# Order changes in a one-core decoder layer: which half of a modulation piece is multiplied first, and where splits, key sums and gate loads stand

## The chip, the cores and the metric

The kernel runs on one core of a Trainium2 chip. The metric is the device time of one launch in microseconds (us), the median of several runs. The core has a matrix engine (TensorE, PE in the profile, with its weight loads on a row PEld), three elementwise engines (VectorE or DVE, ScalarE or ACT, GpSimd or POOL), and a sequencer that mainly issues transfers (SyncE, SP). Each engine works through its own list of instructions in order; they meet through semaphores. Transfers (DMAs) are issued by SP, ACT and POOL.

## The reference

One layer of a decoder for 512 prompt tokens and 8 sample tokens, which share all weights (D = 1024, 16 heads of 64, feed-forward width 2816):

```
sh1, sc1, g1, sh2, sc2, g2 = split(silu(c) @ ada_w + ada_b, 6)
h = rms_norm(x, norm1_g) * (1 + sc1) + sh1
xr, gr, q, k, v, fl, ga, gb = split(h @ w_in)
xc = causal_dwconv(xr);  hr = rg_lru(xc)           # gates: 16 blocks of 64 x 64
ya = (hr * gelu(gr)) @ w_proj_a
yb = attend(q, k, v, log_sigmoid(fl + b_f)) @ w_proj_b
x = x + g1 * ((sigmoid(ga) * ya + sigmoid(gb) * yb) @ w_o)
h2 = rms_norm(x, norm2_g) * (1 + sc2) + sh2
x = x + g2 * ((silu(gu) * up) @ w_ffn_out)         # gu, up = split(h2 @ w_ffn_in)
y = rms_norm(x, normf_g)
```

The prompt attends causally to itself. Each sample token attends to 1024 past rows in pages of 128 rows (`cache_k`, `cache_v`, found through a page table), with a decay from the stored forget values.

## The kernel before

All activations are kept transposed, features on the 128 partitions and the 520 tokens (512 + 8) along the free axis, in two halves of 260. A product of 128 output features is 8 steps over the features of the input, each with three matmuls: weights and activations are both split into a rounded part and the rest (`whi`, `wlo`; `hh`, `hl`), and hi·hi + lo·hi + hi·lo is summed. A weight chunk arrives as `wraw` (L210); for each 128 columns of it, a *unit*, ACT rounds it to `whi` (L246) and DVE subtracts to get `wlo` (L248). `split_upto(n)` (it starts with `while state["split"] <= n`) does this ahead of the product; units 0 and 1 are the weights of q's last two tiles, units 2 and 3 those of the first two tiles of `xr`. `held(m)` puts the subtraction of unit m behind an instruction named in `after[m]`.

The program is written as Python that emits instructions, and a scheduler lays them out per engine by its own estimate of times; `tc.issue_after(i)` tells it to place what follows behind instruction i. That layout is fixed at build time.

Four places matter here.

**q's tiles** (the loop with `q_done`). Tiles 0 to 5 were half computed earlier (`qpart`); their second half goes into a bank `q{i}_{j}`, and DVE adds it to `qp` (L921). `q_done` then copies the 8 sample columns on POOL (L876), writes the tile to DRAM (`qd`, L878) and transposes the sample columns on PE (L879, bank `qt`). After the fourth tile ACT scales the bank (L885) and writes it out as `qtd` (L188). POOL reads it back for one sample, spread over all partitions, as `qb` (L714). In the same loop `forget_logits` (`pfl`), `past_turn` (`lft`), `decay` and `past_conv` (the small `lzc` and `cvp` operations on DVE) are issued.

**Key pages.** POOL issues loads of key pages (`pg`, L696). `key_sum` multiplies a page by `qb` (L740, L744) and sums over each head (L741, L745) on DVE, two DVE instructions of 128x1024 each.

**Gates.** `gate_load(i)` loads the block weights of one tile (`gw`, L903); ACT and DVE split them (L908, L909).

**adaLN pieces.** The modulation for the second half of the layer is `silu(c) @ ada_w`, in 16 pieces (`ada_piece`, L370): two groups `ada1`, `ada2` of 8 input steps. A piece has two loads of 512 KB (`ada_load`, L358, tile `araw`, from a pool of 7 buffers), and each load feeds two matmul calls with 32 output partitions; the four calls of a piece write to four different column groups of the array (`tile_position=(0, 32 * g)`). Each call is two MATMUL records in the trace. The calls are placed among the products `pb` and `wo`; `ada_copy` and `ada_end` turn the sums into `mod`.

Every DMA from SP or ACT raises one of eight semaphores (DMAHW0 to DMAHW7, taken in turn), and waits until the DMA that had the same one before has landed. POOL's DMAs use DMASW0 to DMASW7 in the same way.

Of the kernel before, what the change touches and what calls it, by code (L numbers as in the profile page):

```python
# [12 lines left out]
ALU = mybir.AluOpType  # L13
# [11 lines left out]
KT = 8  # L25
# [3 lines left out]
HALF = NT // 2  # L29
# [36 lines left out]
def kernel(ctx, tc, xT, par, gates, b_f, cst, cse, own, cache_k, cache_v, cache_lf, pt,  # L66
# [3 lines left out]
    pe, act, dve, pool, sp = nc.tensor, nc.scalar, nc.vector, nc.gpsimd, nc.sync  # L70
# [9 lines left out]
    def slot(name, cols=NT, dt=F32, parts=128):  # L80
        return heap.tile([parts, cols], dt, name=name, tag="slot")
# [77 lines left out]
    for jt in range(FF // 128):  # L159
        c = len(chunks)  # L160
# [4 lines left out]
        for name in BLOCKS:  # L165
            units.append((c, name, 4))
            if name in JOIN[jt]:
                g, i = JOIN[jt][name]
# [12 lines left out]
    state = {"n": 0, "dma": 0, "split": 0, "load": 22, "lead": 11, "due": 0, "age": 1}  # L181
# [35 lines left out]
    after = {}  # L217
# [132 lines left out]
    ada_raw = {}  # L350
# [10 lines left out]
    def ada_piece(which, kq):  # L361
        if kq == 0:
            ada_acc[which] = bank(f"ada{which}")
        acc = ada_acc[which]
        if (which, kq) not in ada_raw:
            ada_load(which, kq)
        for g2, raw in enumerate(ada_raw.pop((which, kq))):
            for gg in range(2):
                g = 2 * g2 + gg
                pe.matmul(acc[32 * g:32 * g + 32, :], lhsT=silc[:, kq], rhs=raw[:, gg],  # L370
                          start=kq == 0, stop=kq == KT - 1, tile_position=(0, 32 * g))
# [174 lines left out]
    for f in range(KT):  # L546
        t = slot("sq1")
# [14 lines left out]
    for f in range(KT):  # L562
        t = slot("xn")
# [163 lines left out]
    def key_sums():  # L727
        for p in pend:
            p[0] += 1
        while pend and pend[0][0] >= (state["age"] if state["n"] < 43 else 1000):  # L730
            key_sum()

    def key_sum():
        _, s, j, pg, q, half = pend.pop(0)
        r = s // 2
        c = 256 * (r % 2) + 32 * j + H * (s % 2)
        with tc.issue_after(state["last"].ins):
            if half is not None:
                b, c = 8 * (r % 2) + j, H * (s % 2) + 8 * half
                dve.tensor_tensor(pg, pg, q.unsqueeze(1).to_broadcast([128, 2, 512]), ALU.mult)  # L740
                dve.tensor_reduce(S[r // 2].rearrange("p (b c) -> p b c", c=32)[:, b:b + 2, c:c + 8],  # L741
                                  pg.rearrange("p j (h d) -> p j h d", d=DH), AX.X, ALU.add)
            else:
                dve.tensor_tensor(pg, pg, q, ALU.mult)  # L744
                last = dve.tensor_reduce(S[r // 2][:, c:c + H], pg.rearrange("p (h d) -> p h d", d=DH), AX.X, ALU.add)  # L745
        summed[r] += 1
        if summed[r] == 2 * NPAGE:
            chains.append([9, past_softmax(r)])
        return None if half is not None else last

    def key_pages(n):
        for _ in range(n):
            if keys_todo:
                key_page(*keys_todo.pop(0))
# [119 lines left out]

    def q_done(i, t):
        c = pool.tensor_copy(q8[:, NS * i:NS * i + NS], t[:, NP:])  # L876
        state.setdefault("q8", c)
        sp.dma_start(qd[i], t)  # L878
        pe.transpose(qtp[i // 4][:, 128 * (i % 4):128 * (i % 4) + 128], t[:, NP:], ident)  # L879
        if i % 4 == 3:  # L880
            q_samples(i // 4)
# [17 lines left out]
    gate_raw = {}  # L899

    def gate_load(i):
        gate_raw[i] = slot("gw", 256)
        sp.dma_start(gate_raw[i], gates[i])  # L903

    def gate_split(i):
        gr = gate_raw.pop(i)
# [5 lines left out]
    for i in range(KT):  # L912
        if i % 4 == 0:
            qtp.append(bank(f"qt{i}", NS))
        if i < 6:
            t = qpart[i]
            for j, (t0, t1) in enumerate(HALVES):
                b = bank(f"q{i}_{j}")
                for k in range(4):
                    q_matmuls(1, i, j, k, b)  # L920
                dve.tensor_tensor(t[:, t0:t1], b[:, :HALF], t[:, t0:t1], ALU.add)  # L921
        else:
            t = slot("q")
            product(f"q{i}", h, to(t, act.copy))
        if ready:
            q_done(*ready.pop())
        ready.append((i, t))
        if i == 2:
            flw = forget_weights()
        if i == 3:  # L930
            split_upto(0)
            for n in range(KT):
                gate_load(n)
        if i in (5, 6):
            for n in (2 * i - 10, 2 * i - 9):
                gate_split(n)
        if i == 4:
            with tc.issue_after(state["q8"].ins):
                past_load()
            split_upto(1)  # L940
            load_chunks(1)
            loads[pool] += [state["hr"]] * 4
            key_pages(2)
            with tc.issue_after(state["last"].ins), tc.issue_after(state["act"].ins):
                decay()
                past_conv()
            close = forget_logits(flw)
        if i == 5:
            past_turn(0)
            past_turn(1)  # L950
            key_pages(2)
        if i == 6:
            close()
            load_chunks(2)
        if i == 3:
            q_done(*ready.pop())
    q_last = ready.pop()
# [816 lines left out]
```

## Time and profile before

| what | value |
|---|---|
| runs | 1035.36, 1036.88, 1037.04 us; median 1036.88 |
| the profiled execution's own time | 1032.73 us |
| its span, first to last instruction | 1031.1 us |
| mean granted TensorE clock | 0.995 |
| busy: PE, DVE, ACT, POOL | 1003.5, 794.0, 548.5, 325.1 us |

Rows of the timeline read: start in us from the span's start, duration in us, engine, line, operation, output<-inputs, count, and in brackets the engine's idle time before it with what ended it. Matmuls are pipelined: each record lasts 0.28 us, but in a full stream they start 0.12 us apart, so that the cost of a disturbance is read from the starts. "SPq" and the like are DMA issues. The waits view says who waited for whom: us in total, times, longest. The chain of waits follows the last instruction of a window back through what released each step.

### The profile page before, as it was taken

The page shows a single profiled execution, that of the slowest core. Times are in us where ns is not written, and L with a number is a line of the kernel's source. Part 1 is how long each engine was busy: PE and PEld are TensorE (multiplying, and loading weights), DVE is VectorE, ACT ScalarE, POOL GpSimd, SP SyncE. Part 2 cuts the span into 40 slices and gives each one's busy share as a digit, 9 for nine tenths or more (in the row PEclk, how much of TensorE's full clock was granted, in tenths as well). Part 3 has the DMA queues.
Part 4 walks back from the last instruction along what each step waited for, and adds up shares of the span by engine and source line. Part 5 has one row for each costly group of instructions (what it writes and reads, how often), then busy time and mean ns, then how long its engine had stood idle before and what let it go on. Part 6 is the DMA issues. An engine that isn't in the chain of part 4 may idle for free.

```text
span 1031.1 us, 21277 instructions
## 1 busy us (share of the span) xinstructions
PE 1003.5 (97%) x8012; PEld 923.6 (90%) x8012; DVE 794.0 (77%) x1423; ACT 548.5 (53%) x1128; POOL 325.1 (32%) x416
## 2 busy tenths in 40 slices
PE   5998999999999999999999999999999999999996
PEld 2788999999998988888888877999999999999996
DVE  5548999998999888887655443868878888878865
ACT  4524575847671477777783222555444444445453
POOL 0335211111144146554400000483432433424212
PEclk9999999999999999999999999999999999999998
DMA  9796867778889999987867894324243342333122
GB/s 327 240 318 208 245 228 180 245 247 269 280 260 334 326 320 292 312 271 237 266 199 280 318 341 140 84 63 118 68 124 94 91 123 65 100 103 103 62 63 84
DMA packets 164377, 206.97 MB, mean 201 GB/s; under 512 B 9890, under 2 KB 125106, under 8 KB 164210
## 3 DMA queue, kind: packets, MB, share of 16 engines
q1 hardware_dynamic: 147554, 152.52, 47.6%
q0 software_dynamic: 13040, 46.67, 13.8%
q10 hardware_dynamic: 3680, 6.42, 1.7%
q8 instruction: 63, 1.03, 0.4%
q14 instruction: 40, 0.33, 0.1%
HBM read 192.49 MB, written 13.09 MB: 199 GB/s over the span
## 4 chain that ended last, share of the span: by engine, by line
PE 89%; DMA 4%; DVE 3%; ACT 1%; issue 1%; POOL 1%; SPq 0%; DVEq 0%; POOLq 0%; ACTq 0%
PE fo L305 12%; PE wo L305 5%; PE k L305 5%; PE gb L305 5%; PE gr L305 5%; PE pb L305 5%; PE ga L305 5%; PE v L305 4%; PE xr L305 4%; PE pv L833 3%; PE pa L305 3%; PE ada L370 2%; PE po L1288 2%; PE qp L538 2%; PE ptt L1254 2%; PE fi L305 1%
## 5 line engine op out<-in xcount | busy, mean ns | idle before, releaser
L246 ACT CAST whi<-wraw 128x1024 fp32r<-128x1024 f32 (+1 forms) x79 | 82.0, 1038 | 113.6 <-PE pb L305 34.5
L248 DVE TENSOR_TENSOR wlo<-wraw,whi 128x1024 fp32r<-128x1024 f32 (+1 forms) x79 | 99.6, 1261 | 24.1 <-ACT whi L246 21.8
L270 ACT CAST wb<-ws 128x512 fp32r<-128x512 f32 x72 | 44.8, 622 | 93.5 <-PE fo L305 64.4
L305 PE MATMUL fo<-ach,wb 128*128 128x260 f32 x512 | 93.3, 282 | 0.0
L696 POOL DMA_DIRECT2D pg<-in_cache_k_dram x74 | 39.8, 537 | 151.3 <-DVE S L745 62.5
L271 DVE TENSOR_TENSOR wb<-wraw,wb 128x512 fp32r<-128x512 f32 x86 | 76.6, 891 | 5.7 <-ACT wb L270 4.5
L305 PEld LDWEIGHTS fo<-ach,wb 128*128 128x128 f32 x512 | 79.0, 188 | 0.0
L261 POOL TENSOR_TENSOR ws<-wraw 128x512 f32<-128x512 f32 x18 | 23.9, 1330 | 157.8 <-DMA wraw<-in_w_fi_dram 81.2
L270 ACT CAST wb<-wraw 128x512 fp32r<-128x512 f32 x86 | 53.5, 622 | 36.3 <-ACT cp L1663 6.3
L305 PE MATMUL fo<-acl,wb 128*128 128x260 f32 x256 | 72.3, 282 | 0.0
L271 DVE TENSOR_TENSOR wb<-ws,wb 128x512 fp32r<-128x512 f32 x72 | 59.6, 828 | 14.8 <-ACT wb L270 13.0
L744 DVE TENSOR_TENSOR pg<-pg,qb 128x1024 f32<-128x1024 f32 x48 | 58.0, 1223 | 2.3 <-DMA pg<-in_cache_k_dram 2.2
L745 DVE TENSOR_REDUCE S<-pg 128x16 f32<-128x1024 f32 x48 | 57.3, 1207 | 0.2
L1245 POOL TENSOR_SCALAR p<-p,mu 128x128 f32<-128x128 f32 (+3 forms) x28 | 38.7, 1393 | 51.7 <-DVE mu L1241 45.6
L305 PEld LDWEIGHTS fo<-acl,wb 128*128 128x128 f32 x256 | 48.1, 188 | 0.0
L1239 ACT ACTIVATE p<-p,mu 128x128 f32<-128x128 f32 (+3 forms) x64 | 35.4, 554 | 17.8 <-DVE mu L1238 17.5
L305 PE MATMUL xr<-hh,wlo 128*128 128x260 f32 x128 | 37.1, 290 | 2.1 <-DVE wlo L248 2.1
L305 PE MATMUL v<-hh,whi 128*128 128x260 f32 x128 | 37.3, 291 | 0.8 <-ACT row L813 0.5
L305 PE MATMUL pb<-oh,whi 128*128 128x260 f32 x128 | 37.2, 291 | 0.3 <-ACT oh L1346 0.3
L305 PE MATMUL xr<-hh,whi 128*128 128x260 f32 x128 | 37.4, 292 | 0.0
L305 PE MATMUL k<-hh,whi 128*128 128x260 f32 x128 | 37.3, 291 | 0.0
L305 PE MATMUL gb<-hh,whi 128*128 128x260 f32 x128 | 37.0, 289 | 0.0
(1101 smaller groups left out, 3969.5 us busy)
## 6 DMA issues: line engine op xcount, KB each, us to landing
araw<-in_ada_w_dram SPq DMA_DIRECT2D x48, 512.0 KB, 7.9
wraw<-in_w_fi_dram SPq DMA_DIRECT2D x44, 512.0 KB, 4.2
pg<-in_cache_k_dram POOLq DMA_DIRECT2D x42, 512.0 KB, 6.0
pg<-in_cache_v_dram SPq DMA_DIRECT2D x42, 512.0 KB, 5.4
wraw<-in_w_in_dram SPq DMA_DIRECT2D x34, 512.0 KB, 7.2
wraw<-in_w_in_dram SPq DMA_DIRECT2D x11, 1024.0 KB, 8.8
pg<-in_cache_v_dram POOLq DMA_DIRECT2D x22, 512.0 KB, 6.2
pg<-in_cache_k_dram POOLq DMA_DIRECT2D x32, 256.0 KB, 5.3
```

The costliest lines, as they stand in the source:

```text
L246: state["act"] = act.copy(hi[:, :k1 - k0], src)
L248: state["last"] = dve.tensor_tensor(lo[:, :k1 - k0], src, hi[:, :k1 - k0].bitcast(F32), ALU.subtract)
L261: pool.tensor_tensor(s1, a21, a22, ALU.add)
L270: state["act"] = act.copy(t[:, :4], src)
L271: state["last"] = dve.tensor_tensor(t[:, 4:], src, t[:, :4].bitcast(F32), ALU.subtract)
L305: state["mm"] = pe.matmul(out[:, :t1 - t0], lhsT=wt[k], rhs=at, start=k == 0 and m == 0, stop=k == nk - 1 and m == 2)
L696: done.append(eng.dma_start(pg, cache[bass.ds(r, 1), :, c0:c1].rearrange("a p c -> (a p) c")))
L744: dve.tensor_tensor(pg, pg, q, ALU.mult)
L745: last = dve.tensor_reduce(S[r // 2][:, c:c + H], pg.rearrange("p (h d) -> p h d", d=DH), AX.X, ALU.add)
L833: pe.matmul(pv[0][32 * gq:32 * gq + 32, :], lhsT=pw[r][:, c:c + 32], rhs=pgs[gq // 2][:, 512 * hf:512 * hf + 512], start=j == 0, stop=j == ...
L1239: act.activation(p[:, :n + 128], p[:, :n + 128], AF.Exp, bias=mu[:, 0:1], scale=-1.0, accum_out=mu[:, 1:2])
L1245: (pool.tensor_scalar(p, p, mu[:, 2:3], None, ALU.mult) if a and i + 1 < KT else act.activation(p, p, AF.Copy, scale=mu[:, 2:3]))
```

## The change

Five edits, all of them in the order of things; no operation is added or taken away but that eight gate loads become four.

1. A piece of adaLN multiplies its second load first (`for g2 in (1, 0)`), then its first; before, it took them in the order of loading.
2. The DVE subtractions of units 0 and 1 (q's last two tiles) are put behind the second of the two sums of q's third tile.
3. Key sums are put behind the latest of the sums of q's tiles 0 to 5 (`state["qadd"]`).
4. `past_load` waits as before for the first tile's copy on POOL; four loads of key pages that come after the sixth tile are put behind the copy of the fourth tile.
5. Gates are loaded two at a time, one load of 256 KB each: the first after q's fourth tile, the second after the sixth, the last two after the seventh. Before, all eight loads were issued after the fourth.

```
@@ ada_piece
-        for g2, raw in enumerate(ada_raw.pop((which, kq))):
+        raws_ = ada_raw.pop((which, kq))
+        for g2 in (1, 0):
+            raw = raws_[g2]
             for gg in range(2):
@@ key_sums
-            key_sum()
+            with tc.issue_after(state["qadd"].ins):
+                key_sum()
@@ q_done
-        state.setdefault("q8", c)
+        if i in (0, 3):
+            state["q8"] = c
@@ gate_load
-        gate_raw[i] = slot("gw", 256)
-        sp.dma_start(gate_raw[i], gates[i])
+        t = slot("gw", 512).rearrange("p (g c) -> p g c", g=2)
+        sp.dma_start(t, gates[i:i + 2].rearrange("g p c -> p g c"))
+        gate_raw[i], gate_raw[i + 1] = t[:, 0], t[:, 1]
@@ the loop over q's tiles
-                dve.tensor_tensor(t[:, t0:t1], b[:, :HALF], t[:, t0:t1], ALU.add)
+                state["qadd"] = dve.tensor_tensor(t[:, t0:t1], b[:, :HALF], t[:, t0:t1], ALU.add)
+                if i == 2:
+                    after[0] = after[1] = state["qadd"]
...
+        if i == 1:
+            first_q8 = state["q8"]
...
         if i == 3:
             split_upto(0)
-            for n in range(KT):
-                gate_load(n)
+            gate_load(0)
+        if i == 5:
+            gate_load(2)
...
-            with tc.issue_after(state["q8"].ins):
+            with tc.issue_after(first_q8.ins):
                 past_load()
...
             key_pages(2)
+            loads[pool] += [state["q8"]] * 4
         if i == 6:
             close()
             load_chunks(2)
+            gate_load(4)
+            gate_load(6)
```

What the edits and the scheduler make of it, engine by engine (lines of the changed kernel are 2 to 13 higher):

PE's list is the same up to the product `wo`. There, inside the stream of the `wo` tiles, six of the sixteen adaLN pieces (the last six) stood as two separate pairs of calls; the other ten stood together already. Before, for the first of the six (`araw_9037` and `araw_9039` are its two loads; `x2` in a row stands for two calls):

```order
L305 MATMUL wo1_0_9055<-mixh_8516,whi_8917 128x260
L305 MATMUL wo1_0_9055<-mixh_8516,wlo_8918 128x260
L370 MATMUL ada2_8978<-araw_9037,silc_99 32x512 x2
L305 MATMUL wo1_0_9055<-mixl_8517,whi_8917 128x260
L305 MATMUL wo1_0_9055<-mixh_8591,whi_8917 128x260
L305 MATMUL wo1_0_9055<-mixh_8591,wlo_8918 128x260
L305 MATMUL wo1_0_9055<-mixl_8592,whi_8917 128x260
L305 MATMUL wo1_0_9055<-mixh_8664,whi_8917 128x260
L305 MATMUL wo1_0_9055<-mixh_8664,wlo_8918 128x260
L370 MATMUL ada2_8978<-araw_9039,silc_99 32x512 x2
L305 MATMUL wo1_0_9055<-mixl_8665,whi_8917 128x260
```

And now (`araw_9029` and `araw_9031` are the same two loads):

```order
L305 MATMUL wo1_0_9047<-mixh_8508,whi_8909 128x260
L305 MATMUL wo1_0_9047<-mixh_8508,wlo_8910 128x260
L305 MATMUL wo1_0_9047<-mixl_8509,whi_8909 128x260
L305 MATMUL wo1_0_9047<-mixh_8583,whi_8909 128x260
L305 MATMUL wo1_0_9047<-mixh_8583,wlo_8910 128x260
L305 MATMUL wo1_0_9047<-mixl_8584,whi_8909 128x260
L305 MATMUL wo1_0_9047<-mixh_8656,whi_8909 128x260
L305 MATMUL wo1_0_9047<-mixh_8656,wlo_8910 128x260
L372 MATMUL ada2_8970<-araw_9031,silc_99 32x512 x2
L372 MATMUL ada2_8970<-araw_9029,silc_99 32x512 x2
L305 MATMUL wo1_0_9047<-mixl_8657,whi_8909 128x260
```

The first pair moved down to where the second stood, so that the four calls follow each other. The same happened to the other five.

On DVE the first moved row is that of unit 0's `wlo`: it stood between the sums of q's second and third tile, and stands now between those of the third and the fourth. The second place is around the sums of the sixth tile (`q5_0` and `q5_1` are its two banks, `qp_112` the tile; `pg` and `S` are the key sums, `qb` the spread sample row, `lzc` the small chain of `decay`). Before, from the first instruction that needs `qb`:

```order
L740 TENSOR_TENSOR pg_777<-pg_777,qb_798 128x1024
L609 TENSOR_SCALAR lzc_827<-lzc_827 128x8
L740 TENSOR_TENSOR pg_799<-pg_799,qb_798 128x1024
L608 TENSOR_TENSOR lzc_827<-lzc_827,lzb_826 128x8
L921 TENSOR_TENSOR qp_112<-q5_0_900,qp_112 128x260
L609 TENSOR_SCALAR lzc_827<-lzc_827 128x8
L921 TENSOR_TENSOR qp_112<-q5_1_914,qp_112 128x260
L608 TENSOR_TENSOR lzc_827<-lzc_827,lzb_826 128x8
L740 TENSOR_TENSOR pg_977<-pg_977,qb_798 128x1024
L609 TENSOR_SCALAR lzc_827<-lzc_827 128x8
L741 TENSOR_REDUCE S_775<-pg_777 128x2x8
L610 TENSOR_TENSOR ll_822<-lzc_827,lza_825 128x8
```

Behind these rows came two more sums `S`, a fourth product `pg`, and then `wlo` of unit 2, the first `xr` tile. Now:

```order
L684 TENSOR_SCALAR cneg_578<-le_807 128x8
L926 TENSOR_TENSOR qp_112<-q5_0_886,qp_112 128x260
L926 TENSOR_TENSOR qp_112<-q5_1_900,qp_112 128x260
L743 TENSOR_TENSOR pg_763<-pg_763,qb_784 128x1024
L743 TENSOR_TENSOR pg_785<-pg_785,qb_784 128x1024
L744 TENSOR_REDUCE S_761<-pg_763 128x2x8
L744 TENSOR_REDUCE S_761<-pg_785 128x2x8
L743 TENSOR_TENSOR pg_965<-pg_965,qb_784 128x1024
L743 TENSOR_TENSOR pg_986<-pg_986,qb_784 128x1024
L744 TENSOR_REDUCE S_761<-pg_965 128x2x8
L744 TENSOR_REDUCE S_761<-pg_986 128x2x8
L248 TENSOR_TENSOR wlo_1063<-wraw_759,whi_1062 128x1024
```

The sixth tile's sums now stand ahead of everything that reads `qb`, the chain of `decay` ends before them, and unit 2's `wlo` is behind four whole key sums; before, it was behind four products and three sums.

On SP, from the load of unit 0's chunk (`wraw`), with the semaphores each issue waits for; `qd` are the writes of q's tiles, `gw` the gates. Before:

```order
L210 DMA wraw<-in_w_in_dram 128x8x256 [waits DMAHW6_49,DMAHW7_49,DMAHW1_49,DVE_49]
L878 DMA qd<-qp 128x520 [waits DVE_49]
L903 DMA gw<-in_gates_dram 128x256 [waits DMAHW0_49]
L903 DMA gw<-in_gates_dram 128x256
L903 DMA gw<-in_gates_dram 128x256 [waits DMAHW2_49]
L878 DMA qd<-qp 128x520 [waits DMAHW3_49,DVE_49]
L903 DMA gw<-in_gates_dram 128x256 [waits DMAHW4_49]
L903 DMA gw<-in_gates_dram 128x256 [waits DMAHW5_49]
L903 DMA gw<-in_gates_dram 128x256 [waits DMAHW6_49]
L903 DMA gw<-in_gates_dram 128x256 [waits DMAHW7_49]
L878 DMA qd<-qp 128x520 [waits DMAHW0_49,DVE_49]
L903 DMA gw<-in_gates_dram 128x256 [waits DMAHW1_49]
```

And now:

```order
L210 DMA wraw<-in_w_in_dram 128x8x256 [waits DMAHW6_49,DMAHW7_49,DMAHW1_49,DVE_49]
L882 DMA qd<-qp 128x520 [waits DVE_49]
L907 DMA gw<-in_gates_dram 128x2x256 [waits DMAHW0_49]
L882 DMA qd<-qp 128x520 [waits DVE_49]
L882 DMA qd<-qp 128x520 [waits DMAHW2_49,DVE_49]
L882 DMA qd<-qp 128x520 [waits DMAHW3_49,DVE_49]
L210 DMA wraw<-in_w_in_dram 128x8x256 [waits DMAHW6_49,DMAHW5_49,DVE_49]
L882 DMA qd<-qp 128x520 [waits DVE_49]
L907 DMA gw<-in_gates_dram 128x2x256 [waits DMAHW7_49]
L882 DMA qd<-qp 128x520 [waits DMAHW0_49,DVE_49]
L210 DMA wraw<-in_w_in_dram 128x8x256 [waits DMAHW1_49,DMASW5_49,PE_49]
```

Seven gate loads went away between the writes of q's first four tiles, and the load of the next weight chunk (second `wraw`) moved up behind the fourth write. By the count of DMAs, ACT's write of `qtd` took DMAHW3 before, the semaphore of the second tile's `qd`, and takes now DMAHW4, last used by a load before the first row above. On POOL the load of `qb` is one page load earlier in the list. Later on SP, among the adaLN loads, three `araw` loads moved up by a few rows, one of them ahead of the eight reloads of `x`.

## The prediction

> **What bounds the kernel now.** I read the page's first block, then the waits of PE, then the timeline around each of them.
>
> ```profile
> PE 1003.5 (97%) x8012; PEld 923.6 (90%) x8012; DVE 794.0 (77%) x1423; ACT 548.5 (53%) x1128; POOL 325.1 (32%) x416
> ```
> ```profile
> PE qt L879 <- DVE qp L921: 2.5, 2, 1.7
> PE xr L305 <- DVE wlo L248: 2.1, 2, 1.8
> ```
>
> PE sets the end: it is busy for 97% of the span. These two rows are its only waits of over 1.1 us behind the start, and both lie in q's tiles and the first `xr` tiles. So there are two ways to gain: take these waits away, or make PE's own list shorter. The change touches both.
>
> **The change part by part. First hole.** q's third tile waits for its sums on DVE, and these stood behind the subtraction of unit 0, which waited for its weights:
>
> ```profile
> 62.70 1.23 DVE L248 TENSOR_TENSOR wlo<-wraw,whi 128x1024 fp32r<-128x1024 f32 x1 [5.29 <-ACT whi L246]
> 63.85 1.43 DVE L921 TENSOR_TENSOR qp<-q,qp 128x260 f32<-128x260 f32 x4
> ```
> ```profile
> 64.66 0.27 PE L879 MATMUL qt<-cs,qp 128*8 128x128 f32 x1 [1.73 <-DVE qp L921]
> ...
> 65.33 0.27 PE L879 MATMUL qt<-cs,qp 128*8 128x128 f32 x1
> ```
>
> Queued behind the subtraction were the four sums of the third and fourth tile. Now the third tile's two go ahead, and only the fourth's two are behind it. The weights are ahead of the gates in SP's queue in both kernels, so I leave 62.70 where it is. The fourth tile's sums are then done after two of the four steps of 1.43 / 4 = 0.36, and its transpose starts where the third's started, at 64.66 instead of 65.33. Gain 0.67; of the 1.73 some 1.2 stay, as a wait of the fourth tile's transpose. Should the weights land sooner with fewer loads about, up to that 1.2 comes on top; I take nothing for it.
>
> **Second hole.**
>
> ```profile
> 82.37 0.28 PE L305 MATMUL q<-hl,whi 128*128 128x260 f32 x1
> 83.46 0.27 PE L879 MATMUL qt<-cs,qp 128*8 128x128 f32 x1 [0.81 <-DVE qp L921]
> ```
>
> In a full stream starts are 0.12 us apart, so this hole costs 1.09 - 0.12 = 0.97. The transpose waits for the sixth tile's sums, which stood behind two products with `qb`. The chain of waits shows why `qb` was late:
>
> ```profile
> 57.45 11.51 DMA qd<-qp
> 69.00 0.04 issue
> 69.03 4.42 DMA qtd<-qt
> 73.46 0.02 issue
> 73.50 0.50 issue
> 74.00 6.02 DMA qb<-qtd
> ```
>
> ACT held its write of `qtd` until a write of q's second tile (11.51 us, among the gate loads) had landed. Now the sixth tile's sums stand ahead of everything that reads `qb`. Their banks are full some 8 us before that transpose, and the chain of `decay`, which stands before them, starts earlier too, since ACT is not held until 69. The whole 0.97 goes.
>
> **Third hole, and the clock.**
>
> ```profile
> 90.52 0.37 PE L305 MATMUL xr<-hh,whi 128*128 128x260 f32 x1
> 92.66 0.39 PE L305 MATMUL xr<-hh,wlo 128*128 128x260 f32 x1 [1.77 <-DVE wlo L248]
> 92.89 0.29 PE L305 MATMUL xr<-hl,whi 128*128 128x260 f32 x1
> 93.01 0.36 PE L305 MATMUL xr<-hh,whi 128*128 128x260 f32 x1
> ...
> 96.58 0.28 PE L305 MATMUL xr<-hl,whi 128*128 128x260 f32 x1
> ```
> ```profile
> 93.00:97.00 4.00, 4.00 (x23) 4.00 (x22) 4.00 (x5) 0.52 (x2) 3.37 (x7) 0.57 0.68 214
> ```
>
> 90.52 to 92.89 less two steps is 2.1; a little of it is the usual slow start behind a transpose, so I count 2.0. The second wait in the `xr` row above is 2.1 - 1.8 = 0.3. Behind the hole the granted clock (third number from the end) is 0.57: from 93.01 to 96.58 there are 17 steps, 2.04 us at 0.12; they took 3.57, so 1.53 was lost.
>
> Unit 2's `wlo` moves behind four whole key sums, so what matters is when `qb` lands. ACT's write no longer shares a semaphore with the long `qd`:
>
> ```profile
> 65.64 0.59 ACT L885 ACTIVATE qt<-qt 8x512 f32<-8x512 f32 x1 [1.62 <-PE qt L879]
> ```
>
> Its scaling moves up by the 0.67 and ends at 65.6, and a short operation of 0.2 stands between: issue at 65.8. With the chain's 4.42, 0.50 and 6.02 `qb` lands at 76.7 instead of 80.0. From there DVE needs two blocks of two products and two sums, and the 1.23 of the `wlo`:
>
> ```profile
> 100.47 2.35 DVE L740 TENSOR_TENSOR pg<-pg,qb 128x1024 f32<-128x1024 f32 x2
> 102.74 2.33 DVE L741 TENSOR_REDUCE S<-pg 128x16 f32<-128x1024 f32 x2
> 105.00 1.21 DVE L248 TENSOR_TENSOR wlo<-wraw,whi 128x1024 fp32r<-128x1024 f32 x1
> ```
>
> A block takes 105.00 - 100.47 = 4.53. Unit 2 is ready at 76.7 + 9.06 + 1.23 = 87.0. PE asks for it at 90.72 less the 1.64 gained so far, 89.1: 2.1 to spare. Unit 3 needs two small gate splits (about 1 us), a block and a `wlo` more, 93.7; PE asks 48 steps later, at 94.9: 1.2 to spare, and about as much for the unit behind it. So 2.0 and 0.3 go, and the clock's 1.53 with them if the hole caused it. Beyond 1.2, each us that `qb` is late costs one; for that I take off 0.4. Early part: 0.67 + 0.97 + 2.0 + 0.3 + 1.53 - 0.4 = 5.1 us.
>
> One rule speaks against the clock's share. The Trainium skill, TensorE: Matmul & The Clock Gate (Why this matters for your kernels), lets the clock fall to half after PE has idled for about 3 us. Here a hole of 1.77, eight us behind one of 0.81, went ahead of 0.57, and the 1.73 of the first hole did not, so the trace does not bear the length out. By that rule this hole is too short, something else lowered the clock, and 1.53 stays: a rival below.
>
> **adaLN pieces.** A whole piece and a half one:
>
> ```profile
> 603.47 1.06 PE L370 MATMUL ada<-araw,silc 128*32 128x512 f32 x8
> 604.47 0.39 PE L305 MATMUL wo<-mixh,whi 128*128 128x260 f32 x1
> 604.70 0.28 PE L305 MATMUL wo<-mixh,wlo 128*128 128x260 f32 x1
> ...
> 605.06 0.28 PE L305 MATMUL wo<-mixh,wlo 128*128 128x260 f32 x1
> 605.27 1.05 PE L370 MATMUL ada<-araw,silc 128*32 128x512 f32 x4
> 606.25 0.39 PE L305 MATMUL wo<-mixl,whi 128*128 128x260 f32 x1
> ```
>
> From its start to the next of the stream the whole piece takes 1.00, the half 0.98. Around both, the stream loses 0.09 ahead (605.06 to 605.27 is 0.21) and 0.11 behind (604.47 to 604.70 is 0.23): 1.20 and 1.18. The halves are no cheaper, since the four column groups work side by side. Six pieces stood in halves and now stand whole: 6 x (2 x 1.18 - 1.20) = 6.96 us off PE's own list, in a stretch where it waits for nothing. What this needs is that the loads are there. The tightest piece is the first whose loads are issued behind the last `wo` weights:
>
> ```profile
> 606.93 12.18 SPq L358 DMA_DIRECT2D araw<-in_ada_w_dram  x8
> ```
> ```profile
> DMA to landing us min/median/max: 8.3/8.3/8.3
> ```
> ```profile
> 619.46 1.05 PE L370 MATMUL ada<-araw,silc 128*32 128x512 f32 x4
> ```
>
> Its second load goes out some 0.6 behind 606.93 and lands 8.3 later (the middle row, for the stretch of its issue), at 615.8. PE comes to it at 619.46 less three halves, 615.9; SP's issue hangs on DVE work that lies ahead of the saved halves, so it does not move with PE. That is level; I take off 0.3. The pieces behind it have more. One `araw` load now stands ahead of the reloads of `x` and waits for a buffer until the seventh piece is through, some 5 us; behind it in SP's list is the last `sB`, already late by a little:
>
> ```profile
> 596.93 0.43 DVE L1432 TENSOR_TENSOR sB<-pb,sB 128x260 f32<-128x260 f32 x1 [1.81 <-DMA sB<-sBd]
> ```
>
> PE needs that product in `wo`'s last step, 21 steps behind 600.4, so at 602.9; sum and split behind it end near 602. About 1 us more is covered, and beyond that PE feels it; the queue has as many bytes as before, so I take nothing. This part: 6.7 us.
>
> **Gates in pairs.** The same bytes in four issues less; SP waits for others nearly all this time, and the first gate is split 15 us later. Nothing, covered by SP's slack; without it, 4 issues of about 0.4.
>
> **The sum.** 5.1 + 6.7 = 11.8. The profiled execution took 1032.73, 1.63 more than its span; it becomes 1020.9. The median of the runs shown, 1036.88, lies 4.15 higher; I take the gain over as it is: **1025.1 us**.
>
> **The rivals.** *`qb` lands late.* It shares the queues with a weight chunk, pages and writes, and loads of this kind spread widely:
>
> ```profile
> DMA to landing us min/median/max: 5.4/6.1/9.8
> ```
>
> At 9.8 it lands at 80.5, PE waits 3.8 - 1.2 = 2.6 at unit 3, and the clock may fall again: 4.1 less, but the 0.4 is in already: 1028.8. For it speaks this spread; against it, that seven gate loads have left the queue.
>
> *The clock falls anyway*, as by the rule above: 1.53 less, 1026.6.
>
> *The second load of a piece is late.* At 2.3 us over the 8.3 (the longest of the eight),
>
> ```profile
> DMA to landing us min/median/max: 4.7/9.1/10.6
> ```
>
> the tight piece waits about 2.2: 1027.0.
>
> *Slower.* Taking column groups 2, 3 before 0, 1 might keep the four calls from sharing the array. Then each of the 16 pieces costs two halves, 16 x 2.36 = 37.8, where ten whole and twelve halves now cost 26.2: 11.6 more, less the early 5.1: 1043.4. It turns slower from (26.2 + 5.1) / 16 = 1.96 us per piece. Against it: pairs share already, and no row shows that it matters which comes first. That the change doesn't do what it says is excluded by PE's list, where the halves are together.
>
> **How the numbers follow.** Forecast 0.62, late `qb` 0.14, clock 0.12, late load 0.09, slower 0.03. The forecast's own range is 1023 to 1027.5 (the 1.2 of the first hole on one side, allowances used twice on the other). To hold 8 in 10 I take 1022.3 to 1030, which takes in the first three rivals. Within 0.2%, 2.1 us, this kernel can't be told from no change; the first four cases lie beyond that. Faster 0.95, same 0.02 (several rivals at once), slower 0.03.
>
> **What would show it.** Right: for the last six pieces one group x8 of about 1.06 and none of x4; no wait at the sixth tile's transpose; a first wait of about 1.2 at the fourth's; clock 1.00 from 88 to 97; `qb` read near 77. Wrong: pieces of 2 us, a wait of `ada` for `araw`, `xr` waiting for `wlo`, or `wo` waiting for the last `sB`'s product.

## The result, and the profile after

Five executions of the changed kernel took 1020.05 to 1023.43 us, median **1021.18 us**; five of the kernel before, beside them, 1034.83 to 1037.04, median 1035.97. The ratio is 0.9858, 95% interval 0.9841 to 0.9874: **faster by 14.8 us**. The forecast was 1025.1 with a range down to 1022.3, so the sign is right and the time lies below the range.

The profiled executions say something else. That of after took 1021.18 (span 1019.1, clock 0.997), that of before 1032.73 (span 1031.1): 11.6 us apart, 12.0 by the spans, where the sum said 11.8. The difference between 14.8 and 11.6 is what most of the experiments below are about.

Where the 12.0 lie, by the first block of after's page and rows of TensorE by product (first and last start behind the durations), of before and then of after:

```profile
PE 994.4 (98%) x8012; PEld 920.4 (90%) x8012; DVE 793.0 (78%) x1423; ACT 548.2 (54%) x1128; POOL 329.4 (32%) x416
```
```profile
L305 PE MATMUL ga<-hh,whi x128: 278/282/392, 106.3 to 279.8; 128*128 128x260 f32 x128
L305 PE MATMUL pb<-oh,whi x128: 277/283/389, 542.6 to 598.6; 128*128 128x260 f32 x128
L305 PE MATMUL wo<-mixh,whs x80: 277/282/388, 615.1 to 662.7; 128*128 128x260 f32 x80
```
```profile
L305 PE MATMUL ga<-hh,whi x128: 278/282/388, 100.9 to 274.3; 128*128 128x260 f32 x128
L305 PE MATMUL pb<-oh,whi x128: 277/283/388, 538.3 to 594.1; 128*128 128x260 f32 x128
L305 PE MATMUL wo<-mixh,whs x80: 278/282/388, 608.2 to 651.2; 128*128 128x260 f32 x80
```

At the first `ga` after is 5.4 ahead; 0.8 of that is an earlier start. At the last `pb` it is 4.5 ahead: some 1 us is given back in attention, between 290 and 507, where nothing was edited. From there to the last `wo` it gains 64.1 - 57.1 = 7.0. The rest of the 12.0 is 0.5 at the end.

The early part of after, on TensorE and on VectorE (start, duration, engine, line, operation; the idle time before it and who ended it in brackets):

```profile
62.01 0.27 PE L883 MATMUL qt<-cs,qp 128*8 128x128 f32 x1
...
63.59 0.27 PE L883 MATMUL qt<-cs,qp 128*8 128x128 f32 x1 [0.83 <-DVE qp L926]
...
80.76 0.27 PE L883 MATMUL qt<-cs,qp 128*8 128x128 f32 x1
...
95.12 0.40 PE L305 MATMUL xr<-hh,wlo 128*128 128x260 f32 x1 [1.05 <-DVE wlo L248]
...
598.99 1.06 PE L372 MATMUL ada<-araw,silc 128*32 128x512 f32 x8
599.99 0.39 PE L305 MATMUL wo<-mixh,whi 128*128 128x260 f32 x1
600.21 0.28 PE L305 MATMUL wo<-mixh,wlo 128*128 128x260 f32 x1
```
```profile
76.08 2.48 DVE L743 TENSOR_TENSOR pg<-pg,qb 128x1024 f32<-128x1024 f32 x2 [2.70 <-DMA qb<-qtd]
...
85.63 1.42 DVE L248 TENSOR_TENSOR wlo<-wraw,whi 128x1024 fp32r<-128x1024 f32 x1
...
89.31 2.36 DVE L743 TENSOR_TENSOR pg<-pg,qb 128x1024 f32<-128x1024 f32 x2 [1.37 <-DMA qb<-qtd]
...
93.84 1.22 DVE L248 TENSOR_TENSOR wlo<-wraw,whi 128x1024 fp32r<-128x1024 f32 x1
```

Three things are to be seen. The third and the sixth tile's transposes (62.01, 80.76) wait for nothing, the fourth's waits 0.83. `qb` is read at 76.08 and unit 2 is ready at 87.05: forecast 76.7 and 87.0. Unit 3 is late: TensorE waits 1.05 for it at 95.12, where no wait was forecast, because the pages ahead of it on VectorE waited for a *second* `qb`. GpSimd issued that one only at 84.95, behind a row of suffix sums:

```profile
80.15 4.87 POOL L456 TENSOR_TENSOR after<-after,lk 128x64 f32<-128x64 f32 x7
84.95 0.55 POOL L716 DMA_DIRECT2D qb<-qtd  x1
```

### The profile page after: what moved, and what is told of

Same layout as the page of the kernel before. It is cut to its first block, busy times and chain, and to the rows that moved or that the text cites. A ratio compares the mean times of both kernels' runs of the same rounds, so it can differ in the third digit from the quotient of the medians.

```text
span 1019.1 us, 21277 instructions
## 1 busy us (share of the span) xinstructions
PE 994.4 (98%) x8012; PEld 920.4 (90%) x8012; DVE 793.0 (78%) x1423; ACT 548.2 (54%) x1128; POOL 329.4 (32%) x416
## 3 DMA queue, kind: packets, MB, share of 16 engines
q0 software_dynamic: 13040, 46.67, 13.9%
## 4 chain that ended last, share of the span: by engine, by line
PE 89%; DMA 4%; DVE 2%; ACT 1%; issue 1%; POOL 1%; POOLq 0%; SPq 0%; DVEq 0%; ACTq 0%
PE fo L305 12%; PE k L305 5%; PE wo L305 5%; PE gb L305 5%; PE gr L305 5%; PE ga L305 5%; PE pb L305 5%; PE v L305 4%; PE xr L305 4%; PE pv L836 3%; PE pa L305 3%; PE po L1301 2%; PE qp L540 2%; PE ada L372 2%; PE ptt L1267 2%; PE fi L305 1%
## 5 line engine op out<-in xcount | busy, mean ns | idle before, releaser
L271 DVE TENSOR_TENSOR wb<-ws,wb 128x512 fp32r<-128x512 f32 x72 | 64.4, 894 | 14.1 <-ACT wb L270 12.2
```

The lines of the kernel that those rows point to most:

```text
L271: state["last"] = dve.tensor_tensor(t[:, 4:], src, t[:, :4].bitcast(F32), ALU.subtract)
```

## The experiments

The four kernels of a group ran on one chip beside the kernel before; each group has its own runs of before (medians 1035.82, 1035.97, 1035.04, 1035.38; the second and the fourth group on the same chip).

### Where an ordinary execution of before loses more than its profiled one

The kernel before again, then each half of the change alone, and a version of after with both of its remaining waits attacked. The edits of the last three:

```diff
# adaLN alone, on before
-        for g2, raw in enumerate(ada_raw.pop((which, kq))):
+        raws_ = ada_raw.pop((which, kq))
+        for g2 in (1, 0):
+            raw = raws_[g2]
# early edits alone: after, with these lines put back
# both waits, on after
-                if i == 2:
+                if i == 3:
                     after[0] = after[1] = state["qadd"]
...
-            qb[0] = slot("qb", 512)
+            qb[0] = qb.pop(1) if s == 1 and half == 0 else slot("qb", 512)
...
+            qb[1] = slot("qb", 512)
+            pool.dma_start(qb[1], qtd[1:2, :512].partition_broadcast(128))
             past_turn(0)
             past_turn(1)
```

> The kernel before, unchanged, to see how its ordinary executions differ from the profiled one (1032.73 us, span 1031.1, mean clock 0.995), which lies 2.1 us below the lowest of its five timed runs. Theory A (the early waits are longer in ordinary runs, and the clock falls more behind them): spans of about 1034, mean clock 0.991 to 0.993 in most runs, median near 1036, and if its profile is an ordinary one, a larger loss between 60 and 100 us. Theory B (the half pieces of adaLN cost more in ordinary runs): the clock stays at 0.995, and the loss lies in the stretch of wo. Theory C (nothing lies in the kernel, the first profile had a lucky start): the clock stays at 0.995, and spans differ by when the first work of TensorE begins.

> Before, with only the order of the two loads in an adaLN piece changed. The last six pieces stand whole, by the profile 7.0 us off TensorE's list. Theory A: 1036 - 7.0 = 1029.0, and the early part as before. Theory B: 7.0 plus the 3.3 by which the medians of before exceed its profile, 1025.7. Theory C: 1029, with the remaining gain shared by chance.

> After, with the order of the two loads in an adaLN piece put back, so that the early edits stand alone. Theory A: the gain of the medians less adaLN's, 14.8 - 7.0 = 7.8, so 1028.2, mean clock 0.997. Theory B and C: the 4.7 that the two profiles show between the third tile of q and unit 3, so 1031.3.

> After, with units 0 and 1 behind q's fourth tile's sums in place of the third's, and the second load of qb issued on GpSimd ahead of its two runs of suffix sums. What remains in after's early part is a wait of 0.83 us at the fourth tile's transpose and one of 1.05 at unit 3, for pages that wait for the second qb, issued at 84.95 behind 4.87 us of those sums. If these two are the whole price: 1021.2 - 1.9 = 1019.3, and neither wait is in the profile. Rival: the waits move on (the fifth tile's sums stand behind two subtractions of 1.2 us each, or unit 2's subtraction gets later), 1021.

Measured: before again 1036.57 (1032.59 to 1039.19); adaLN alone 1029.07, ratio 0.9934 (0.9919 to 0.9949); early edits alone 1031.04 (1026.74 to 1036.43), ratio 0.9954 (0.9934 to 0.9974); both waits 1020.93, ratio 0.9840 (0.9825 to 0.9855).

The profile of before taken here is an ordinary execution (1036.48, span 1034.8, clock 0.993), and its early part does not look like the one the forecast was made from. Its waits of TensorE, SyncE's issue of the weight chunk that holds units 0 and 1, ScalarE's first use of it, and busy time by stretch of time (TensorE first, the granted clock third from the end):

```profile
PE qt L879 <- DVE qp L921: 6.8, 1, 6.8
PE xr L305 <- DVE wlo L248: 1.6, 1, 1.6
```
```profile
52.01 0.39 SPq L210 DMA_DIRECT2D wraw<-in_w_in_dram  x1
```
```profile
65.94 1.99 ACT L246 CAST whi<-wraw 128x1024 fp32r<-128x1024 f32 x2 [13.00 <-DMA wraw<-in_w_in_dram]
```
```profile
60.77:64.18 3.41, 1.42 (x12) 1.21 (x11) 0.00 (x0) 0.00 (x0) 0.00 (x0) 1.00 1.03 223
64.18:74.42 10.24, 5.45 (x26) 5.37 (x27) 4.13 (x7) 4.17 (x6) 2.00 (x5) 0.50 0.81 246
```

The same two rows in the first profile of before:

```profile
52.75 0.39 SPq L210 DMA_DIRECT2D wraw<-in_w_in_dram  x1
```
```profile
61.62 1.05 ACT L246 CAST whi<-wraw 128x1024 fp32r<-128x1024 f32 x1 [7.94 <-DMA wraw<-in_w_in_dram]
```

From issue to first use the chunk took 13.9 us here and 8.9 there. The wait of the third tile's transpose grew with it from 1.73 to 6.8, and from inside that wait on (64.18) the clock stood at 0.50 for 10.2 us. The sixth tile then waits for nothing: a long first hole hides the second. Theory A fits before: the loss stands between 60 and 75 us, the clock falls there, and only 7 of its 83 executions in this study were as short as the profiled one. The profile of adaLN alone, whose early part is before's, shows the same: chunk 14.1, wait 6.9, and 10.2 us at 0.50 from 64.57.

For the split of the gain: adaLN alone is worth 6.8 (5.3 to 8.4), the early edits alone 4.8 (2.7 to 6.8), together 11.6. So theory A's 7.8 for the early part, which was the 14.8 less adaLN, was wrong, and the first difference of 14.8 is more than its parts.

The version with both waits attacked lies 0.25 us under the first median of after, not the 1.9 of its expectation. The fourth tile's wait is gone and unit 3 waits 0.20, but unit 2 now waits 0.72: a part of the waiting moved on, as its rival said.

### The gate loads

After again, and three variants: gates as eight early single loads (after), as single loads at the late places (after), and the late pairs alone (before).

```diff
# gates early, on after (single loads, all behind the fourth tile)
-            gate_load(0)
-        if i == 5:
-            gate_load(2)
+            for n in range(KT):
+                gate_load(n)
...
-            gate_load(4)
-            gate_load(6)
# singles late, on after: gate_load(0), (1) at i == 3; (2), (3) at i == 5; (4) to (7) at i == 6
# gates only, on before: the change's gate_load and its three places, nothing else
```

> The kernel after, unchanged, beside the three below. Theory G (the gate loads share the DMA engines with the weight chunk of units 0 and 1 when they are issued together with it; the change's gain in an ordinary run comes from sending them later): the chunk's load takes 8.5 to 10 us, the wait at the fourth tile's transpose is 0.8 to 2.2 us, median 1021 to 1024. Rival P (the two edits ahead of the sums on DVE are what counts, as I predicted, and gates are worth nothing): the same median; the rows below tell the two apart.

> After, with the eight gate loads put back as single loads behind the fourth tile; the other edits stay. Theory G: the chunk takes 13 to 14 us as in the ordinary run of before, unit 0's subtraction starts at 66 to 67, the fourth tile's transpose waits some 5 us, the clock falls behind that to 0.50 for several us; the later hole at unit 3 closes: 1021 + 4.5 + 2.5 - 1 = 1027. Rival P: no change, 1021.

> After, with eight single gate loads, but at the three places where the pairs stand. Theory G (only the moment counts): as after, within 0.2 per cent. Rival P2 (it is the number of loads): a part of the loss of early gate loads, 1023 to 1025.

> Before, with the gate loads in pairs at the three late places and nothing else. Theory G: the chunk takes 8.5 to 10 us, the third tile's transpose waits about 2 in place of 6.8, the clock stays up there; the waits of the sixth tile and of unit 2 return as in the first profile: 1031 to 1033. Rival P: 1036, no change.

Measured: after again 1023.91 (1020.45 to 1029.48), ratio 0.9888 (0.9854 to 0.9922); gates early 1024.68; singles late 1022.29; gates only 1033.1, ratio 0.9968 (0.9948 to 0.9987).

Theory G falls where it was most definite. With the gates early the chunk took 10.7, not 13 to 14; with them late it took 11.1 in after again here, and 12.6 and 13.5 in two later profiles. What makes this load take 8.6 to 14.1 us from one execution to the next is not settled. The gates alone don't decide it: with them early it took 8.9, 10.7, 13.9 and 14.1, with them late 8.6 to 13.5. The three versions of after can't be told apart.

Yet on before the gates alone gained 3.3 us by the ratio (1.3 to 5.4), close to theory G's number, but not in theory G's way: in its profile the chunk took 11.3, the third tile waited 4.2, and the clock fell for 3.41 us at 67.85. The chain of waits names another way in which the gates can act. With early gates ScalarE's write of `qtd` is held by a write of q's second tile; so it was in the first profile (11.51, quoted in the forecast), and so it is again with gates early on after:

```profile
57.18 12.19 DMA qd<-qp
69.44 4.03 DMA qtd<-qt
```

With late gates `qtd` follows ScalarE's scaling directly (64.53 behind 63.91 + 0.59 in after). But in the ordinary profile of before, with its long first hole, the write was not held either, early gates or not:

```profile
70.47 0.59 ACT L885 ACTIVATE qt<-qt 8x512 f32<-8x512 f32 x1 [2.54 <-PE qt L879]
71.08 0.55 ACTq L188 DMA_DIRECT2D qtd<-qt  x1
```

So how much of the 3.3 comes by `qtd` isn't shown, and its cause stays open.

### The hold on units 0 and 1

Before, with these two subtractions behind the fourth tile's sums and nothing else; after again; and after with the hold moved to the fifth and to the fourth tile.

```diff
# before, hold only
-                dve.tensor_tensor(t[:, t0:t1], b[:, :HALF], t[:, t0:t1], ALU.add)
+                state["qadd"] = dve.tensor_tensor(t[:, t0:t1], b[:, :HALF], t[:, t0:t1], ALU.add)
+                if i == 3:
+                    after[0] = after[1] = state["qadd"]
# fifth tile, on after (with the early second qb of above)
-                if i == 2:
+                if i == 4:
# fourth tile, on after: this one line and nothing else
-                if i == 2:
+                if i == 3:
```

> Before, with the subtractions of units 0 and 1 behind the fourth tile's sums and nothing else. Theory H (an ordinary execution of before loses its 3 to 4 us over the profiled one at the third tile's transpose, because the sums stand behind a subtraction whose weight chunk lands 8.8 to 14 us after its issue; the same chain is what remains in after): no wait at the third and the fourth tile however late the chunk is, the clock stays up there, and what is left is the chain of the first profile by qd, qtd and qb (unit 2 at 92.7): 1032 to 1033. Rival (the loss is in the transfers themselves and only moves on): 1036.

> After, unchanged, as the measure for the two below on the same chip: 1021 to 1024 by its two results so far.

> After, with the subtractions of units 0 and 1 behind the fifth tile's sums, and the second qb issued ahead of GpSimd's suffix sums. Theory H: neither the fourth nor the fifth tile's sums can be held by a late chunk, so the spread closes and the median falls by the 0.8 to 3.4 us that after waits at the fourth tile: 1019 to 1020.5, clock 0.997. Rival: the chunk's buffer comes free later, the next weights go out later and unit 2 waits: 1022 or more.

> After, with the subtractions of units 0 and 1 behind the fourth tile's sums, the second qb left where it is. Theory H: no wait at the fourth tile, the wait of about 1 at unit 3 back: 1020.5 to 1022. Rival (the second qb was what counted in the version with both): as after.

Measured: hold alone on before 1034.72, ratio 0.9998 (0.9986 to 1.0011); after 1023.51 (1020.23 to 1026.85), 0.9893 (0.9868 to 0.9918); fifth tile 1026.96; fourth tile **1020.75** (1019.49 to 1021.71), 0.9863 (0.9841 to 0.9885).

Theory H's number for before was wrong, and the rival's "only moves on" came nearer. The profile shows one way to lose it again, in a short execution (1033.30, the second lowest of twelve). The waits, the chain, and the stretches around the new hole:

```profile
PE qt L879 <- DVE qp L921: 2.9, 1, 2.9
```
```profile
57.76 14.98 DMA qd<-qp
...
72.82 2.91 DMA qtd<-qt
...
76.28 4.23 DMA qb<-qtd
```
```profile
80.03:83.44 3.41, 1.06 (x9) 0.85 (x8) 2.81 (x6) 3.39 (x8) 0.00 (x0) 1.00 0.35 131
83.44:86.85 3.41, 2.90 (x8) 1.26 (x9) 3.41 (x9) 0.94 (x2) 2.79 (x7) 0.50 0.57 138
86.85:90.27 3.42, 3.42 (x18) 3.42 (x17) 3.42 (x6) 0.00 (x0) 3.40 (x10) 0.50 1.02 354
```

The wait at the third tile is gone and stands at the sixth, at 83.94, with the clock at 0.50 for 6.8 us from 83.44 on. By the two profiles, two chains of near length end in before's early part: chunk, subtraction, sums; and `qd`, `qtd`, `qb`, key products, sums. Cutting the first alone gave nothing by the ratio. In after, where the second is shorter, moving the hold to the same place gains 2.8 us on after's own median and closes its spread.

The kernel for the fifth tile did not do what its expectation says: unit 0's split is written at the fourth tile, before the hold exists, so it stood ahead of the third tile's sums as in before, and only unit 1 moved. Its waits are those of that order, and the rival's as well, since the next chunk went out late (at 72.55, where after's first profile has 64.70):

```profile
PE ga L305 <- DVE wlo L248: 4.1, 1, 4.1
PE qt L883 <- DVE qp L926: 3.4, 1, 3.4
```

The version with the early second `qb` (1020.93) can't be told from the one without it. In its profile unit 3 waits 0.20, where the second profile of the fourth-tile version, below, has 1.22; that gain of 1 us is smaller than these medians can show.

### Each early edit undone, and both versions again

```diff
# no splits, on after
-                if i == 2:
-                    after[0] = after[1] = state["qadd"]
# no keys, on after
-            with tc.issue_after(state["qadd"].ins):
-                key_sum()
+            key_sum()
```

> After, unchanged, on the chip of the three below. Theory M (the first median of 1021.18 was five executions with an early weight chunk, out of a spread of 1020 to 1029.5): 1022.5 to 1024.5 again. Rival (the chips differ): 1021.

> After, with the subtractions of units 0 and 1 behind the fourth tile's sums, a second time. Theory M (the spread of after is the wait of the fourth tile's sums for that chunk, and the clock behind it): 1020 to 1021.5, and no execution over 1022.5. Rival (the first result was the chip): as after.

> After, with units 0 and 1 ahead of the third tile's sums again; keys, gates and adaLN as in after. By my prediction's step this is worth 0.67 (two of four sums of 0.36), so after plus 0.7. Rival (the third tile's transpose holds a longer tail, as where unit 1 alone was moved): after plus 3.

> After, with the key sums free to stand ahead of the sixth tile's sums, as before. By my prediction's step the sixth tile then waits for qb and two products: qb is read at 76.1 to 78.1 in after, the sums are done some 5 us later at 81 to 83, and TensorE asks for them near 80.8 to 82: a wait of 0.3 to 1.5, and unit 2 gets later by nothing, since the same key work lies ahead of it; after plus 0.3 to 1.5. Rival (the key work ahead of unit 2 gets longer by the mixing and the wait at unit 2 returns, the clock falls): after plus 3 to 5.

Measured: after 1025.48 (1021.39 to 1027.3), ratio 0.9894 (0.9874 to 0.9913); hold at the fourth tile **1021.48** (1019.54 to 1022.11), 0.9860 (0.9838 to 0.9883); no splits 1025.65; no keys 1023.5.

After's own profile is now one with a late chunk, 12.6 us from issue to use, and the fourth tile waits 4.8. In the version with the hold at the fourth tile the chunk was late too, 11.2, and no transpose waits; what is left is 2.5 at units 2 and 3 in two pieces (1.30 at 88.47, 1.22 at 95.83), neither with a clock fall behind it. Of after the issue, the first use and the wait; of the other the same:

```profile
52.84 0.39 SPq L210 DMA_DIRECT2D wraw<-in_w_in_dram  x1
```
```profile
65.43 1.99 ACT L246 CAST whi<-wraw 128x1024 fp32r<-128x1024 f32 x2 [11.65 <-DMA wraw<-in_w_in_dram]
```
```profile
PE qt L883 <- DVE qp L926: 4.8, 1, 4.8
```
```profile
51.87 0.39 SPq L210 DMA_DIRECT2D wraw<-in_w_in_dram  x1
```
```profile
63.09 2.00 ACT L246 CAST whi<-wraw 128x1024 fp32r<-128x1024 f32 x2 [10.28 <-DMA wraw<-in_w_in_dram]
```
```profile
PE xr L305 <- DVE wlo L248: 2.5, 2, 1.3
```

So theory M holds for the hold at the fourth tile, and in kind for after, whose median here lies 1 us above the range given. The 23 executions of after on four occasions run from 1020.05 to 1029.48, median 1023.46; the first five lie at the lower end of that. Whether by chance or by the chip isn't told by these runs; on one and the same chip two medians were 1023.91 and 1025.48. The nine of the version with the hold at the fourth tile run from 1019.49 to 1022.11, median 1021.14: 2.3 less than after's 23, and 2.8 and 4.0 less than after beside them on the same chips. By the ratios of the three later occasions (0.9888, 0.9893, 0.9894) the change is worth 11.0 to 11.6 us, not 14.8.

That after's spread arises ahead of the first `ga`, and hardly behind it, is seen from its other three profiles, of spans 1021.3, 1022.3 and 1025.6. Their first `ga` start 1.7, 3.0 and 5.5 us later than the 100.9 of the first profile, and their spans are 2.2, 3.2 and 6.5 longer:

```profile
L305 PE MATMUL ga<-hh,whi x128: 278/282/388, 102.6 to 276.0; 128*128 128x260 f32 x128
L305 PE MATMUL ga<-hh,whi x128: 278/282/388, 103.9 to 277.3; 128*128 128x260 f32 x128
L305 PE MATMUL ga<-hh,whi x128: 278/282/388, 106.4 to 279.8; 128*128 128x260 f32 x128
```

*No splits* gives 0.2 more than after, far within its spread. Its worth shows better in the profiles, where the wait at the transpose goes with the chunk's time (issue to first use) along two lines:

| order | chunk, us | wait of the transpose, us | chunk less wait |
|---|---|---|---|
| third tile waits (before, twice; adaLN alone; gates only; fifth tile; no splits) | 8.87, 13.93, 14.09, 11.31, 10.54, 13.47 | 1.73, 6.79, 6.94, 4.16, 3.39, 6.31 | 7.14 to 7.16 |
| fourth tile waits (after, four times; early edits alone; gates early; singles late; no keys) | 8.56, 11.13, 9.25, 12.59, 9.92, 10.70, 9.29, 9.89 | 0.83, 3.38, 1.51, 4.84, 2.18, 2.95, 1.55, 2.14 | 7.73 to 7.75 |

In the other four profiles, those with the hold at the fourth tile, neither of the two transposes waits. Each us of the chunk beyond the last column is a us of waiting. The split edit is worth the distance of the lines, 0.6.

*No keys* gave 1023.5, in the middle of after's executions, and its sixth tile doesn't wait. On VectorE the sums again stand between two products, and on TensorE the transpose asks later than that:

```profile
77.02 1.23 DVE L742 TENSOR_TENSOR pg<-pg,qb 128x1024 f32<-128x1024 f32 x1 [4.88 <-DMA qb<-qtd]
78.24 0.42 DVE L925 TENSOR_TENSOR qp<-q,qp 128x260 f32<-128x260 f32 x1
78.65 1.22 DVE L742 TENSOR_TENSOR pg<-pg,qb 128x1024 f32<-128x1024 f32 x1
79.86 0.42 DVE L925 TENSOR_TENSOR qp<-q,qp 128x260 f32<-128x260 f32 x1
```
```profile
82.11 0.27 PE L882 MATMUL qt<-cs,qp 128*8 128x128 f32 x1
```

With `qb` read at 77 the sums are done at 80.3, 1.8 ahead of the question. Here the key edit covers a case that the earlier `qb` already covers; without it but with a late `qb` the sixth tile did wait, 0.81 and 2.9 us, in the first profile of before and in the hold on before.

## Where the prediction was right, and where it was wrong

**adaLN (forecast 6.7): right, 7.0.** From the last `pb` to the last `wo` every profile with the old order has 64.0 to 64.1 us, every one with the new 57.1 to 57.2, in all eighteen profiles. That is the 6.96 of the sum; the 0.3 taken off for a late second load was not needed, since no piece waited. Alone it measured 6.8. The rival that the column groups stop sharing falls: the pieces are x8 and last 1.06.

**First hole (0.67): right in size, wrong in what it was read from.** The two lines of the table are 0.6 apart. But the profile with the 1.73 was an execution with an early chunk. The step said that the subtraction's start stays "where it is", as if 62.70 were a property of the order; it is that of one transfer, and in the next profile of before it was 67.02.

**Second hole (0.97): right in that profile, for another reason than given.** The wait is gone, but without the key edit it is gone too. With the `qb` of that profile, read at 77, the sums are done in time, and where the first hole is long nothing is left to gain there.

**Third hole, second `xr` wait, clock (2.0, 0.3, 1.53, less 0.4): mostly right.** Of the 5.1 for the early part the two profiles show 5.4 at the first `ga` less the 0.8 of the start, 4.6. `qb`, unit 2 and the clock of 1.00 from 88 to 97 came as forecast. Unit 3's 0.3 was a loss of 0.76: the step counted "a block and a `wlo`" and overlooked that this block reads a second `qb`, which before had issued at 85.58 and after issues at 84.95. It stands behind suffix sums that take 0.70 apiece there.

**Gates ("Nothing, covered by SP's slack"): mis-attributed.** The earlier `qb` was in the sum, credited to ScalarE's write no longer being held by `qd`. That release hangs on the gate edit: with the gates early again, `qd` takes 12.19 and holds `qtd` until 69.44. So this edit carries a part of what the sum booked elsewhere. Alone on before it gained 3.3 (1.3 to 5.4); which part of that is this release isn't shown.

**The step that failed** is the last line of the sum: the median "lies 4.15 higher; I take the gain over as it is". It treats the distance from profile to median as a constant of the kernel. In after the runs show it to be a wait: for a chunk that takes 8.6 to 14.1 us, and, where that is long, for the half clock behind it; with the subtractions behind the fourth tile's sums most of the spread is gone. For before it rests on two profiles, its own second one and that of adaLN alone, and the hold alone did not remove it there. In before the distance is 3.15 (1035.88, the median of all 83 executions, less 1032.73); in after, over all 23, it is 2.3 over a profile with an early chunk; in the five executions of the result, none.

So the 3.9 us between 1025.1 and 1021.18 are these: 1.0 because 1036.88, of three executions, lies above the 1035.88; 0.6 because after's distance is shorter than before's, 2.3 against 3.15, less the 0.25 by which after's profile is over the sum's 1020.9; and 2.3 because the five executions lie low in after's spread, which is no step of the sum. The later medians of after, 1023.51 to 1025.48, lie inside the range. A range for a median of five needed that spread below it as well, down to about 1020.

**Luck.** That the two profiles lie 11.6 apart, where the sum said 11.8, is in part luck. Both had an early chunk (8.87 and 8.56 us); the second profile of before and the last of after, with late ones (13.93 and 12.59), are 9.2 apart. And the sum's agreement holds a start that was 0.8 earlier, 1 us given back in attention and 0.5 gained at the end, none of which it has.

## What to carry to other kernels

When a profiled execution lies outside the timed ones, the first question is which wait it does not have: look for a transfer on the path whose duration is one draw from a wide spread, and price the edit at both ends. An engine that works in order should not take up an operation that waits for a transfer while sums stand behind it that another engine needs sooner; held until behind them, a transfer of up to 11.2 us held up no transpose here, and most of the spread went with it. And where two chains of near length end at one place, an edit to one of them can measure nothing alone, as the hold on before did, and 2.8 us with the other chain shorter; it is judged in both places.

## What the runs showed of the hardware

The granted clock changes on a fixed grid. Its eleven falls in the early part of the profiles lasted 3.41 (five times), 6.83 (four times) and 10.24 us (twice): one, two and three times 3.41; and from the fall behind a hole to the last one, at the kernel's end, are 931.84 us in the first profile of before (93.07 to 1024.91) and 965.97 in the second (64.18 to 1030.15), 273.0 and 283.0 times 3.413. So the length of a hole alone does not decide; where it lies on the grid is part of it. The hole of 1.77 left 1.64 us of work in its step, and the clock fell; that of 1.73 left 1.69, and it stayed. A hole of 2.95 that lay across two steps left 2.40 and 1.47, and the clock stayed, in the profile with early gates on after:

```profile
60.86:64.27 3.41, 2.40 (x21) 2.17 (x19) 0.02 (x1) 1.09 (x2) 0.54 (x1) 1.00 1.06 254
64.27:67.68 3.41, 1.47 (x13) 1.47 (x14) 3.20 (x5) 1.59 (x3) 1.30 (x2) 1.00 1.04 353
```

The last row does not fit a bound near half a step, since 1.64 was too little elsewhere. Five of the eighteen profiles have one more fall of 3.41 us, in attention, starting between 462.7 and 466.4 us, and there TensorE's busy time in the step ahead of it was 2.79 to 2.90 us. So busy time alone does not give the bound, and what is counted stays open. On the way up a step with 2.90 us of work, the second of the three quoted from the hold on before, still kept the clock at 0.50.

The Trainium skill, TensorE: Matmul & The Clock Gate (What's actually happening), gives a free-running window of 3413 ns; the traces agree with it to the third digit. The rule of about 3 us of idle time that the forecast took from the same page, as speaking against the clock's share, does not hold in these traces: 1.77 us was enough and 2.95 was not.
